# Hybrid encoder trunk: heavy and light experts strictly in turn, two more weight places, tables in small parts

## The chip, the cores and the metric

The kernel runs on one core of one Trainium2 chip. The metric is the time of one execution in device microseconds, lower is better. Times of a stage are counted from the first instruction of the profiled execution.

## What is computed

Two residual layers over 1024 tokens of width 1024. Each has a token mixer (layer 0: differential and latent attention side by side; layer 1: neighbourhood attention) and a mixture of 32 gated experts, and after both a layer norm. The change touches the mixture alone:

```python
grp = argmax(softmax(xt @ w_rg + b_rg))                     # 4 groups of 8 experts
top_v, top_i = top_k(e_logits of that group, 2)             # two experts per token
gate = softmax(top_v) * g_w
def block(tids, e, w):                                      # up to 128 tokens of one expert
    xb = x_pad[tids]
    hdn = silu(xb @ w1[e]) * (xb @ w3[e])                   # 1024 -> 512, twice
    return (hdn @ w2[e]) * w                                # 512 -> 1024
out = segment_sum(y, slot_tok)
```

All arrays are float32. An expert has 6 MB of weights (w1, w3, w2), a layer 192 MB, read once per execution.

## The kernel before

A layer first does its attention and output projection (`out_project`), on whose last rows the router works. Then `moe` walks through the 32 experts, one step `s` per expert. Experts are ranked by their number of tokens; a rank has a fixed room of slots (`ROOM`, 176 down to 24). Ranks 0 to 13, and rank 31, are heavy: 128 slots at a time, as three products of a split operand (each float32 operand as a rounded part `hi` and a rest `lo`, lines 164 to 169). Ranks 14 to 29, and 30, are light: 64 or 32 slots, plain float32 products straight from the loaded weights (`pair`, line 1165), two or four of them side by side on the array. The four largest ranks have an extra light block for what is over 128. Ranks 30 and 31 stand for the fixed experts 0 and 1; their weights can be loaded before the ranking is known.

A step has rounds `i` = 0 to 7 for gate and up of expert `s`, then 8 to 11 for the down product of expert `s - 1`. In between, at fixed rounds, stand the transposes of the next expert's tokens (`turn`, tiles `xs` or `xh`, `xl`), of the hidden row (`turn_hidden`, tiles `hs` or `hh`, `hl`), the gathers of tokens and the scatters of results. Instructions of TensorE, VectorE, ScalarE and GpSimd run in the order in which the code emits them; SyncE's queue is ordered by a scheduler, and works in that order.

For a heavy expert each 1 MB load is split into `hi` (ScalarE, line 2082) and `lo` (VectorE, line 2083) in two halves, called pieces; there are five places for pieces and the code splits three ahead (`fill`). A heavy expert's load place is free when its second piece is split, a light one's when TensorE has read it.

`Experts` sets the order of the experts (`order`: two fixed, `LEAD` light ones, then heavy ones with light ones spread between, `TRAIL` light ones last) and the list of 192 loads (`flow`). Loads go to SyncE's queue in that order (`load`, line 2103), each waiting for its place: nine common places (`raw`), shared with the output projection, and two more (`mw2`). The last 14 loads use the nine alone. The loads of expert numbers that only the ranking knows need a register, read by SyncE (line 2100).

`overflow_tables` (line 1337 on) computes tables for tokens beyond the room of their expert, all on VectorE; it is a generator, and `moe` calls `next(over)` in each round from step 8 on until it ends. It gives way three times.

Of the kernel before, what the change touches and what calls it, by code (L numbers as in the profile page):

```python
# [18 lines left out]
P = 128  # L19
# [20 lines left out]

FIRST_MORE = 6
LEAD, TRAIL, TURN = 1, 2, 6
# [92 lines left out]
class Kernel:  # L135
# [960 lines left out]
    def moe(self, layer, ahead):  # L1096
# [3 lines left out]
        with ExitStack() as st:  # L1100
# [33 lines left out]
            def turn(p):  # L1134
                for b, n, at in self.blocks(order[p]):
                    if n < P:
                        pt = flat(psT.tile([P, 4, P], F32, name="tp", tag="tp")).rearrange("p (c s) -> p c s", c=NC)
                        for c in range(NC):
                            nc.tensor.transpose(pt[:, c, 0:n], gx[b][at:at + n, c::NC], self.ident[at:at + n, at:at + n])  # L1139
                        xts[b] = pr.tile([P, NC, 64], F32, name="xs", bufs=3)[:, :, 0:n]  # L1140
                        nc.scalar.activation(xts[b], pt[:, :, 0:n], AF.Copy)  # L1141
                        continue
                    hi, lo = xts[b] = pr.tile([P, NC, P], F32R, name="xh"), pr.tile([P, NC, P], F32R, name="xl")
                    for g in range(2):
                        pt = psT.tile([P, 4, P], F32, name="tp", tag="tp")
                        for j in range(4):
                            c = 4 * g + j
                            nc.tensor.transpose(pt[:, j, 0:n], gx[b][0:n, c::NC], self.ident[0:n, 0:n])
                        self.split(hi[:, 4 * g:4 * g + 4], lo[:, 4 * g:4 * g + 4], pt[:, :, 0:n])

# [39 lines left out]
            def turn_hidden(p):  # L1190
                for b, n, _ in self.blocks(order[p]):
                    pt = psT.tile([P, 4, P], F32, name="tp", tag="tp")
                    for j in range(4):
                        nc.tensor.transpose(pt[:, j], hs[b][:, j::4], self.ident)  # L1194
                    if n == P:
                        hts[b] = [pr.tile([P, 4, P], F32R, name="hh"), pr.tile([P, 4, P], F32R, name="hl")]
                        self.split(hts[b][0], hts[b][1], pt)
                    else:

                        h = pr.tile([P, 4, 64], F32, name="hs", bufs=3)  # L1200
# [45 lines left out]
            turn(0)  # L1246
            for s in range(NE + 1):
                if s < NE:
# [5 lines left out]
                    for i in range(8):  # L1254
# [82 lines left out]
    def overflow_tables(self, keep, pr):  # L1337
# [8 lines left out]
        V.tensor_tensor(m, over[:, :, None].to_broadcast([P, NE, NT]), t[:, None, 0:NT].to_broadcast([P, NE, NT]), op=OP.is_gt)  # L1346
        blocks = kk([NE], "oblk")
        V.tensor_reduce(blocks, m, axis=AX.X, op=OP.add)
        end = blocks
        for d in (1, 2, 4, 8, 16):  # L1350
# [3 lines left out]
            end = e  # L1354
        begin = kk([NE], "obegin")
# [5 lines left out]
        for i in range(2):  # L1361
            m = pr.tile([P, NT, NE], F32, name="rt", tag="gs", bufs=1)
            at, st = kk([NT], "oat%d" % i), kk([NT], "ost%d" % i)
            V.tensor_tensor(m, self.ch[i], cap[:, None].to_broadcast([P, NT, NE]), op=OP.mult)
            V.tensor_reduce(at, m, axis=AX.X, op=OP.add)
            V.tensor_tensor(at, self.po[i], at, op=OP.subtract)
            V.tensor_tensor(m, self.ch[i], begin[:, None].to_broadcast([P, NT, NE]), op=OP.mult)
            V.tensor_reduce(st, m, axis=AX.X, op=OP.add)
            V.scalar_tensor_tensor(st, st, float(P), at, op0=OP.mult, op1=OP.add)
# [597 lines left out]
class Experts:  # L1967
# [3 lines left out]
    def __init__(self, k, layer, side):  # L1971
# [4 lines left out]
        self.more, self.first_more = None, FIRST_MORE  # L1976
# [58 lines left out]
    def tile(self, shape, name="raw"):  # L2035

        more = self.of_more()
        self.count += 1
        if more:
            return self.more.tile(shape, F32, name=name, tag="raw", bufs=RAWS2)  # L2040
        return self.raw(shape, name)

    def of_more(self):
        i = self.count - self.first_more
        return i >= 0 and i % (RAWS + RAWS2) < RAWS2 and self.count + 1 < len(self.flow) - TAIL

    def follow(self):

        while self.done < len(self.flow):
            held = self.held.get(self.of_more(), [])  # L2050
            n = RAWS2 if self.of_more() else RAWS
# [36 lines left out]
    def load(self, upto, mark=None):  # L2088
        k, nc = self.k, self.k.nc
        while self.done < min(upto, len(self.flow)):  # L2090
            p, j = self.flow[self.done]
            r = self.order[p]
            more = self.of_more()
# [54 lines left out]
```

## Time and profile before

| | |
|---|---|
| median of 3 runs | 2553.79 us (2548.26 to 2555.2) |
| profiled execution | 2551.09 us, of it span 2549.3 us |
| TensorE / VectorE / ScalarE busy | 2352.0 / 1601.5 / 1209.1 us |
| experts of layer 0: first and last product | 776.26, 1339.29 us |
| experts of layer 1: first and last product | 1941.47, 2496.17 us |

A share of busy time is an average over stages with different limits; the two expert stages are read on their own below. The granted clock is given as a share of full speed: 1.00 is 2.4 GHz, 0.50 is 1.2 GHz. The DMA share is the mean busy share of the core's 16 DMA engines, and can come out a little over 1.

### The profile page before, as it was taken

Reading aid. Unit: us, or ns where it says so; the run is one execution under the profiler, and the core shown is the slowest. Engines: PE = TensorE matmul, PEld = TensorE weight load, DVE = VectorE, ACT = ScalarE, POOL = GpSimd, SP = SyncE. Lnnn points to the kernel's source line nnn. Section 1 sums busy time; section 2 is a strip of 40 time slices with the busy share of each in tenths; the row PEclk is TensorE's granted clock in tenths of the full one; section 3 lists DMA queues with packets and bytes.
Section 4 is the critical chain, followed back from the end, with each engine's and each line's share of the span. In section 5 each row is a group of like instructions: output and inputs, shape, how many; then the busy total and the mean of one; then the engine's idle time right before and its main releaser. Section 6 shows DMA issues by size and latency. Waiting matters only on the chain. (4 is left out here: it accounts for less than half of the span.)

```text
span 2549.3 us, 34566 instructions
## 1 busy us (share of the span) xinstructions
PE 2352.0 (92%) x11972; PEld 1691.2 (66%) x11972; DVE 1601.5 (63%) x2923; ACT 1209.1 (47%) x2093; POOL 484.6 (19%) x513
## 2 busy tenths in 40 slices
PE   8998999999988999999986999999897999999991
PEld 8786777887774655656535878888784665666640
DVE  4328878888575665656645346676676565656656
ACT  3217866777213534444424346666413443444433
POOL 0006752332001111111111012222001111111112
PEclk9999999999998989999997999999998999999995
DMA  4105412000626898999996564545735898999996
GB/s 147 40 17 100 87 39 75 1 1 25 241 101 229 336 391 336 395 406 409 391 402 234 163 147 126 127 127 157 250 115 181 306 392 358 404 402 416 402 414 245
DMA packets 179754, 582.12 MB, mean 228 GB/s; under 512 B 32728, under 2 KB 91112, under 8 KB 128632
## 3 DMA queue, kind: packets, MB, share of 16 engines
q1 hardware_dynamic: 165880, 546.29, 59.1%
q0 software_dynamic: 13696, 33.58, 3.7%
q8 instruction: 97, 1.59, 0.2%
q14 instruction: 81, 0.66, 0.1%
HBM read 518.61 MB, written 56.05 MB: 225 GB/s over the span
## 5 line engine op out<-in xcount | busy, mean ns | idle before, releaser
L2083 DVE TENSOR_TENSOR lo<-raw,hi 128x1024 fp32r<-128x1024 f32 x360 | 423.9, 1222 | 84.3 <-ACT hi L2082 79.2
L2082 ACT ACTIVATE hi<-raw 128x1024 fp32r<-128x1024 f32 x360 | 363.7, 1057 | 43.2 <-PE hy L169 34.1
L1165 PE MATMUL hy<-raw,xs 128*64 128x512 f32 (+1 forms) x1408 | 302.3, 615 | 7.0 <-DMA raw<-in_w_up_dram 3.1
L1232 POOL DMA_INDIRECT y_scratch<-xg,msi x72 | 71.8, 997 | 895.2 <-DVE xg L1226 767.8
L1226 DVE SCALAR_TENSOR_TENSOR xg<-hy,mgate,xg 128x512 f32<-128x512 f32 (+2 forms) x172 | 125.3, 745 | 129.0 <-PE hy L1165 115.8
L168 PE MATMUL hy<-lo,xh 128*128 128x512 f32 x480 | 190.0, 396 | 8.2 <-DVE lo L2083 8.2
L167 PE MATMUL hy<-hi,xh 128*128 128x512 f32 x480 | 197.1, 411 | 0.0
L169 PE MATMUL hy<-hi,xl 128*128 128x512 f32 x480 | 189.6, 395 | 0.0
L1165 PEld LDWEIGHTS hy<-raw,xs 128*64 128x64 f32 (+1 forms) x1408 | 80.4, 132 | 159.4 <-issue 137.0
L1165 PE MATMUL hy<-raw,hs 128*64 128x512 f32 (+1 forms) x704 | 144.8, 608 | 11.7 <-DMA raw<-in_w_down_dram 10.2
L161 DVE TENSOR_TENSOR pl<-tp,ph 128x512 fp32r<-128x512 f32 x192 | 129.9, 680 | 23.9 <-ACT ph L160 23.8
L160 ACT ACTIVATE ph<-tp 128x512 fp32r<-128x512 f32 x192 | 112.3, 595 | 40.6 <-PE tp L664 23.4
L167 PE MATMUL o<-whi,xh 128*128 128x512 f32 (+1 forms) x320 | 126.5, 395 | 2.6 <-ACT whi L160 2.5
L168 PE MATMUL o<-wlo,xh 128*128 128x512 f32 (+1 forms) x320 | 125.6, 392 | 1.6 <-DVE wlo L161 1.6
L169 PE MATMUL o<-whi,xl 128*128 128x512 f32 (+1 forms) x320 | 124.7, 390 | 2.2 <-DVE xl L152 2.2
L167 PEld LDWEIGHTS hy<-hi,xh 128*128 128x128 f32 x480 | 91.4, 190 | 33.5 <-issue 10.0
L1764 POOL TENSOR_SCALAR e<-e,sm 128x288 f32<-128x288 f32 (+1 forms) x128 | 68.7, 549 | 218.5 <-DVE sm L1763 202.0
L161 DVE TENSOR_TENSOR pt<-tp,pt 96x384 fp32r<-96x384 f32 (+1 forms) x128 | 65.2, 549 | 70.9 <-ACT pt L160 69.5
L168 PEld LDWEIGHTS hy<-lo,xh 128*128 128x128 f32 x480 | 91.2, 190 | 27.6 <-DVE lo L2083 11.3
L151 ACT ACTIVATE hh<-tp 128x512 fp32r<-128x512 f32 x30 | 17.9, 597 | 185.5 <-PE tp L1194 185.5
L657 POOL TENSOR_SCALAR e<-e,sm 128x1024 f32<-128x1024 f32 x64 | 72.1, 1126 | 177.5 <-DVE sm L656 111.9
L1141 ACT ACTIVATE xs<-tp 128x512 f32<-128x512 f32 (+1 forms) x44 | 23.4, 537 | 173.0 <-PE tp L1139 173.0
(429 smaller groups left out, 5578.3 us busy)
## 6 DMA issues: line engine op xcount, KB each, us to landing
raw<-in_w_gate_dram SPq DMA_DIRECT2D x128, 1024.0 KB, 14.9
raw<-in_w_up_dram SPq DMA_DIRECT2D x128, 1024.0 KB, 13.3
raw<-in_w_down_dram SPq DMA_DIRECT2D x128, 1024.0 KB, 14.6
y<-y_scratch SPq DMA_DIRECT2D x14, 1024.0 KB, 13.1
v_scratch<-vst SPq DMA_DIRECT2D x32, 256.0 KB, 3.4
raw<-in_odd_w_qkv_dram SPq DMA_DIRECT2D x16, 512.0 KB, 5.4
vw<-v_scratch SPq DMA_DIRECT2D x16, 512.0 KB, 4.9
x_scratch<-z SPq DMA_DIRECT2D x14, 512.0 KB, 2.8
```

Source lines behind the costliest of these rows:

```text
L160: nc.scalar.activation(hi, src, AF.Copy)
L161: return lambda: nc.vector.tensor_tensor(lo, src, as32(hi), op=OP.subtract)
L167: mm(out, l[0], r[0], start=start, stop=False)
L168: mm(out, l[0], r[1], start=False, stop=False)
L169: mm(out, l[1], r[0], start=False, stop=stop)
L657: nc.gpsimd.tensor_scalar(e, e, sm[:, 3:4], 1.0, op0=OP.mult, op1=OP.mult)
L1165: mm(out[at:at + n], x[:, k], ws(k)[i], start=k == z, stop=k == nk - q + z, tile_position=(0, at))
L1226: nc.vector.scalar_tensor_tensor(x, y, gate, x, op0=OP.mult, op1=OP.add))
L1232: nc.gpsimd.indirect_dma_start(out=self.y_dram, out_offset=bass.IndirectOffsetOnAxis(ap=slot(b, n)[1], axis=0), in_=yo[0:n], in_offset=Non ...
L1764: nc.gpsimd.tensor_scalar(e, e, sm[:, 2:3], 1.0, op0=OP.mult, op1=OP.mult)
L2082: nc.scalar.activation(hi, src, AF.Copy)
L2083: nc.vector.tensor_tensor(lo, src, as32(hi), op=OP.subtract)
```

## The change

The order of the experts becomes (H heavy, L light; B one of the four largest, with an extra block):

```
before  L H L B H L H L H L B L H L H L H L B L H L H L B L H L H L L L
after   L H L B L H L H L H L B L H L H L H L B L H L H L B L H L H L L
```

`TRAIL` goes from 2 to 1. The places `xh`, `xl`, `hh` and `hl` go from two to one each, `xs` and `hs` from three to two. A third pool `mw3` of two 1 MB places opens in the same room of memory; of 13 loads 9 go to the common places, 2 to `mw2`, 2 to `mw3`. The twelve static loads no longer wait for the ranking; the first load by number waits for the last activation of `turn(0)`. `overflow_tables` gives way fourteen times, and is called in every second round from step 4 on.

```diff
-LEAD, TRAIL, TURN = 1, 2, 6
+RAWS3, THIRD = 2, 5
+LEAD, TRAIL, TURN = 1, 1, 6
...
-            ex.load(ex.static - 2)
-            ex.load(ex.static, self.ranked)
             pr = self.pool("mr", bufs=2, ctx=mr, side="right")
+            ex.third = self.pool("mw3", bufs=RAWS3, ctx=mr, side="right")
+            ex.load(ex.static)
...
-                    hi, lo = xts[b] = pr.tile([P, NC, P], F32R, name="xh"), pr.tile([P, NC, P], F32R, name="xl")
+                    hi, lo = xts[b] = [pr.tile([P, NC, P], F32R, name=x, bufs=1) for x in ("xh", "xl")]
...
-                        hts[b] = [pr.tile([P, 4, P], F32R, name="hh"), pr.tile([P, 4, P], F32R, name="hl")]
+                        hts[b] = [pr.tile([P, 4, P], F32R, name=x, bufs=1) for x in ("hh", "hl")]
...
-            turn(0)
+            ex.load(ex.static + 1, turn(0))
...
-                        elif s >= 8:
+                        elif s >= 4 and i % 2:
                             next(over, None)
...
+    def which(self):
+        i = self.count - self.first_more
+        if i < 0 or self.count + 1 >= len(self.flow) - TAIL:
+            return 0
+        i %= RAWS + RAWS2 + RAWS3
+        return 1 if i < RAWS2 else 2 if THIRD <= i < THIRD + RAWS3 else 0
```

Three places show how instructions move. The first is SyncE's queue at the start of the experts of layer 0 (`x_scratch<-z` writes the last token rows that the first gathers read; `idsi` holds the ranked expert numbers). Before:

```order
L2103 DMA raw<-in_w_down_dram 128x2048 [waits PE_49]
L2103 DMA raw<-in_w_down_dram 128x2048 [waits DMAHW2_49,PE_49]
L849 DMA x_scratch<-z 128x512 [waits DVE_49,Pool_49]
L849 DMA x_scratch<-z 128x512 [waits DMAHW4_49,Pool_49]
L2103 DMA raw<-in_w_down_dram 128x2048 [waits DVE_49,PE_49]
L2100 TENSOR_LOAD idsi [waits DVE_49]
```

After:

```order
L2119 DMA raw<-in_w_down_dram 128x2048 [waits PE_49]
L2119 DMA raw<-in_w_down_dram 128x2048 [waits DMAHW2_49,PE_49]
L2119 DMA raw<-in_w_down_dram 128x2048 [waits PE_49]
L851 DMA x_scratch<-z 128x512 [waits DMAHW4_49,DVE_49,Pool_49]
L851 DMA x_scratch<-z 128x512 [waits Pool_49]
L2119 DMA raw<-in_w_down_dram 128x2048 [waits DMAHW6_49,Activation_49]
L2116 TENSOR_LOAD idsi [waits DVE_49]
```

The third load moves ahead of the writes of z, and the fourth from behind 15 reads of numbers to ahead of all of them; the first load by number, which stood behind 15 reads, stands behind 23.

The second is VectorE where the tables begin (`lo` is a piece's rest, `xg` the sum of a result, `hl` and `xl` the rests of a heavy expert's operands). Before, in step 8:

```order
L2083 TENSOR_TENSOR lo<-raw,hi 128x1024 x5
L1343 TENSOR_TENSOR over<-total,cap 128x32
L1345 TENSOR_SCALAR capt<-iota 128x8
L1346 TENSOR_TENSOR rt<-over,capt 128x256
L1348 TENSOR_REDUCE oblk<-rt 128x32
L1352 COPY oend_8681<-oblk 128x1
L1353 TENSOR_TENSOR oend_8681<-oblk 128x31
```

After, in step 4:

```order
L1186 TENSOR_TENSOR hg<-hg,hy 128x512
L1347 TENSOR_TENSOR over<-total,cap 128x32
L1349 TENSOR_SCALAR capt<-iota 128x8
L1350 TENSOR_TENSOR rt<-over,capt 128x256
L1229 SCALAR_TENSOR_TENSOR xg_7394<-hy,mgate,xg_7394 64x512 x2
L154 TENSOR_TENSOR hl<-tp,hh 128x512
L1214 TENSOR_TENSOR hs<-hs,tp 128x256
L1353 TENSOR_REDUCE oblk<-rt 128x32
L1357 COPY oend_8117<-oblk 128x1
L1358 TENSOR_TENSOR oend_8117<-oblk 128x31
```

Sixteen instructions stood in one block; now three stand alone, and other work of the step comes before the next part.

The third is TensorE at the end of the experts of layer 0 (`xs` and `hs` are the light operands, `hg` a hidden row, `xg` a token row). Before:

```order
L1165 MATMUL hy<-raw,xs 32x512 x4
L1194 MATMUL tp<-ident,hg 128x128 x4
L1165 MATMUL hy<-raw,xs 32x512 x8
L1139 MATMUL tp<-ident,xg_7394 128x32 x8
L1165 MATMUL hy<-raw,xs 32x512 x4
L1165 MATMUL hy<-raw,hs 32x512 x8
L1165 MATMUL hy<-raw,xs 32x512 x4
L1194 MATMUL tp<-ident,hg 128x128 x4
L1165 MATMUL hy<-raw,xs 32x512 x12
L1165 MATMUL hy<-raw,hs 32x512 x4
L1194 MATMUL tp<-ident,hg 128x128 x4
L1165 MATMUL hy<-raw,hs 32x512 x12
```

After:

```order
L169 MATMUL hy<-hi,hh 128x512
L170 MATMUL hy<-lo,hh 128x512
L171 MATMUL hy<-hi,hl 128x512
L1168 MATMUL hy<-raw,xs 32x512 x4
L1197 MATMUL tp<-ident,hg 128x128 x4
L1168 MATMUL hy<-raw,xs 32x512 x12
L1168 MATMUL hy<-raw,hs 32x512 x4
L1197 MATMUL tp<-ident,hg 128x128 x4
L1168 MATMUL hy<-raw,hs 32x512 x12
```

The down products of the last heavy expert now end one light expert later in the list, so two light experts' products follow its gate and up instead of three.

## Rows read from the trace of the kernel before

**Rows 1.** Busy time by stretches, layer 0; the first line names the columns

```profile
core 0: us, PE busy (x) PEld busy (x) DVE busy (x) ACT busy (x) POOL busy (x), PEclk, DMA share, GB/s
796.00:816.00 20.00, 20.00 (x100) 13.53 (x100) 8.12 (x19) 6.98 (x10) 2.89 (x3) 1.00 0.74 258
...
840.00:860.00 20.00, 20.00 (x93) 10.64 (x92) 11.65 (x13) 9.74 (x12) 2.40 (x2) 1.00 0.61 219
...
942.00:948.00 6.00, 6.00 (x19) 4.23 (x19) 1.04 (x1) 1.08 (x2) 0.00 (x0) 0.50 1.01 418
948.00:954.00 6.00, 6.00 (x23) 1.86 (x24) 1.44 (x2) 0.00 (x0) 0.00 (x0) 0.76 0.74 267
...
980.00:1000.00 20.00, 20.00 (x98) 10.08 (x96) 3.97 (x6) 4.31 (x7) 1.95 (x2) 1.00 0.68 259
1020.00:1260.00 240.00, 238.05 (x1153) 145.49 (x1151) 149.24 (x162) 111.59 (x142) 37.02 (x32) 0.99 1.01 401
1284.00:1340.00 56.00, 43.88 (x244) 17.41 (x242) 22.37 (x30) 11.29 (x20) 6.05 (x6) 0.91 1.00 401
```

**Rows 2.** ScalarE in order of time: start, duration, instruction, idle before

```profile
1025.88 0.59 ACT L1182 ACTIVATE hg<-hy 128x512 f32<-128x512 f32 x1
...
1038.04 1.08 ACT L151 ACTIVATE xh<-tp 128x512 fp32r<-128x512 f32 x2 [1.65 <-PE tp L1148]
...
1056.70 0.59 ACT L1182 ACTIVATE hg<-hy 128x512 f32<-128x512 f32 x1
```

**Rows 3.** Weight loads issued from 1020 to 1260 us, by line

```profile
L2103 SPq DMA_DIRECT2D raw<-in_w_up_dram x29: 332/333/333, 1020.1 to 1256.6; - x29
...
L2103 SPq DMA_DIRECT2D raw<-in_w_gate_dram x29: 332/333/1117, 1022.4 to 1258.9; - x29
...
L2103 SPq DMA_DIRECT2D raw<-in_w_down_dram x28: 332/333/336, 1030.6 to 1249.4; - x28
```

**Rows 4.** Busy time by stretches, layer 1

```profile
1976.00:2040.00 64.00, 63.02 (x301) 38.63 (x300) 38.41 (x41) 30.65 (x39) 6.39 (x6) 1.00 0.82 307
...
2104.00:2108.00 4.00, 2.84 (x6) 1.74 (x6) 3.76 (x11) 0.00 (x0) 3.26 (x3) 0.57 1.01 428
...
2440.00:2497.00 57.00, 46.68 (x259) 21.45 (x257) 24.87 (x35) 13.18 (x23) 7.58 (x7) 0.91 0.93 385
```

**Rows 5.** VectorE in order of time, first and last of 34 table instructions

```profile
928.66 0.18 DVE L1343 TENSOR_TENSOR over<-total,cap 128x32 f32<-128x32 f32 x1
...
940.55 0.17 DVE L1372 TENSOR_SCALAR oat<-oat 128x8 f32<-128x8 f32 x1
```

**Rows 6.** TensorE in order of time, waits for pieces in both layers

```profile
938.16 0.80 PE L168 MATMUL hy<-lo,xh 128*128 128x512 f32 x1 [2.95 <-DVE lo L2083]
...
941.96 0.79 PE L168 MATMUL hy<-lo,xh 128*128 128x512 f32 x1 [0.87 <-DVE lo L2083]
...
2104.40 0.71 PE L168 MATMUL hy<-lo,xh 128*128 128x512 f32 x1 [2.93 <-DVE lo L2083]
...
2108.20 0.50 PE L168 MATMUL hy<-lo,xh 128*128 128x512 f32 x1 [0.96 <-DVE lo L2083]
```

**Rows 7.** SyncE's queue in order of time, start of layer 0's experts

```profile
768.37 10.78 SPq L2103 DMA_DIRECT2D raw<-in_w_down_dram  x2
```

**Rows 8.** SyncE's reads of expert numbers, both layers: ns min/median/max

```profile
L2100 SPq TENSOR_LOAD <-idsi x60: 260/266/477, 770.0 to 1954.8; - x60
L2100 SPq FUSED_REGOPS  x60: 147/147/192, 770.5 to 1955.2; - x60
```

**Rows 9.** TensorE's last four waits in each layer, first and last

```profile
1329.92 1.07 PE L1165 MATMUL hy<-raw,hs 128*32 128x512 f32 x8 [0.68 <-DMA raw<-in_w_down_dram]
...
1337.35 1.94 PE L1165 MATMUL hy<-raw,hs 128*32 128x512 f32 x8 [1.37 <-DMA raw<-in_w_down_dram]
...
2487.80 1.06 PE L1165 MATMUL hy<-raw,hs 128*32 128x512 f32 x8 [0.62 <-DMA raw<-in_w_down_dram]
...
2495.11 1.06 PE L1165 MATMUL hy<-raw,hs 128*32 128x512 f32 x8 [1.32 <-DMA raw<-in_w_down_dram]
```

More of the change, by code (lines that the diff above doesn't have):

```diff
@@ L1134, in turn @@
             def turn(p):
+                mark = None
                 for b, n, at in self.blocks(order[p]):
@@ L1139, in turn @@
                             nc.tensor.transpose(pt[:, c, 0:n], gx[b][at:at + n, c::NC], self.ident[at:at + n, at:at + n])
[L1140 to L1141 removed]
+                        xts[b] = pr.tile([P, NC, 64], F32, name="xs", bufs=2)[:, :, 0:n]
+                        mark = nc.scalar.activation(xts[b], pt[:, :, 0:n], AF.Copy)
                         continue
[L1143 removed]
+                    hi, lo = xts[b] = [pr.tile([P, NC, P], F32R, name=x, bufs=1) for x in ("xh", "xl")]
                     for g in range(2):
@@ L1149, in turn @@
                         self.split(hi[:, 4 * g:4 * g + 4], lo[:, 4 * g:4 * g + 4], pt[:, :, 0:n])
+                return mark
             def product(out, x, c, w, start, stop):
@@ L1346, in overflow_tables @@
         V.tensor_tensor(m, over[:, :, None].to_broadcast([P, NE, NT]), t[:, None, 0:NT].to_broadcast([P, NE, NT]), op=OP.is_gt)
+        yield
         blocks = kk([NE], "oblk")
@@ L1354, in overflow_tables @@
             end = e
+            if d in (2, 8):
+                yield
         begin = kk([NE], "obegin")
@@ L1364, in overflow_tables @@
             V.tensor_tensor(m, self.ch[i], cap[:, None].to_broadcast([P, NT, NE]), op=OP.mult)
+            yield
             V.tensor_reduce(at, m, axis=AX.X, op=OP.add)
             V.tensor_tensor(at, self.po[i], at, op=OP.subtract)
+            yield
             V.tensor_tensor(m, self.ch[i], begin[:, None].to_broadcast([P, NT, NE]), op=OP.mult)
+            yield
             V.tensor_reduce(st, m, axis=AX.X, op=OP.add)
+            yield
             V.scalar_tensor_tensor(st, st, float(P), at, op0=OP.mult, op1=OP.add)
@@ L1975, in __init__ @@
         self.pool = k.pool("mw", bufs=RAWS, ctx=self.ctx, side=side)
-        self.more, self.first_more = None, FIRST_MORE
+        self.more, self.first_more, self.third = None, FIRST_MORE, None
         self.pieces, self.filled, self.halves = {}, 0, {}
@@ L2035, in tile @@
     def tile(self, shape, name="raw"):
-        more = self.of_more()
+        which = self.which()
         self.count += 1
-        if more:
-            return self.more.tile(shape, F32, name=name, tag="raw", bufs=RAWS2)
+        if which:
+            pool, n = ((self.more, RAWS2), (self.third, RAWS3))[which - 1]
+            return pool.tile(shape, F32, name=name, tag="raw", bufs=n)
         return self.raw(shape, name)
-    def of_more(self):
+    def which(self):
         i = self.count - self.first_more
-        return i >= 0 and i % (RAWS + RAWS2) < RAWS2 and self.count + 1 < len(self.flow) - TAIL
+        if i < 0 or self.count + 1 >= len(self.flow) - TAIL:
+            return 0
+        i %= RAWS + RAWS2 + RAWS3
+        return 1 if i < RAWS2 else 2 if THIRD <= i < THIRD + RAWS3 else 0
     def follow(self):
         while self.done < len(self.flow):
-            held = self.held.get(self.of_more(), [])
-            n = RAWS2 if self.of_more() else RAWS
+            held = self.held.get(self.which(), [])
+            n = (RAWS, RAWS2, RAWS3)[self.which()]
             if len(held) >= n and held[-n] not in self.used:
@@ L2092, in load @@
             r = self.order[p]
-            more = self.of_more()
+            more = self.which()
             t = self.tile([P, 4, 512] if j < 4 else [P, 2, D])
```

2 lines of the change are left out of this document (1 added, 1 removed).

## Prediction

> **What bounds the kernel now.** I read the page's first two parts, then the busy time by stretches, then who waits in the stretches where TensorE is not busy, then the weight loads' own issues. Nearly all of the change lies in the two expert stages (layer 0: 776 to 1339 us, layer 1: 1941 to 2496 us), so only they are priced.
>
> Inside a stage two engines are almost equally loaded. TensorE is busy in 238.05 of the 240 us from 1020 to 1260 while the DMA share is 1.01 [rows 1]. One heavy and one light expert take TensorE 30.8 us there, by the silu of two heavy experts that follow each other [rows 2]; they need twelve 1 MB loads. In the same 240 us 29 + 29 + 28 = 86 loads are issued [rows 3], one per 2.79 us, so twelve take 33.5 us. The stream of weights is therefore the slower of the two by 2.7 us a pair, and lives on the lead it had before 1020. When that is gone TensorE waits: from 1284 to 1340 it is busy 43.88 of 56 us [rows 1], in layer 1 46.68 of 57 us [rows 4]. The lead could have been larger: the DMA share is 0.74, 0.61 and 0.68 in 796-816, 840-860 and 980-1000 [rows 1], 5.2 + 7.8 + 6.4 = 19.4 us idle with work to do; layer 1 idles 0.18 x 64 = 11.5 us in 1976-2040 alone [rows 4]. In these stretches the loads wait for places, that is for TensorE. A lead gained early is spent late, microsecond for microsecond, until TensorE itself has no waits left.
>
> **The change part by part.**
>
> *Tables in fifteen parts.* Before, all of it stands in the first three rounds of step 8, a heavy expert: between 928.66 and 940.72 us VectorE works off 34 small instructions [rows 5], in three blocks, and the subtractions that TensorE needs stand behind them. TensorE waits 2.95 + 0.87 us in layer 0 and 2.93 + 0.96 us in layer 1 [rows 6]. Its clock then falls: granted 0.50 in 942-948 and 0.76 in 948-954, TensorE busy throughout [rows 1], 3.0 + 1.4 = 4.4 us of work lost; in layer 1 0.57 in 2104-2108 with 2.84 us busy [rows 4], 1.2 us. After, the parts hang on every second round of steps 4 to 7, at most about 1 us each. VectorE's cover: it is busy 149.24 of 240 us [rows 1], so four steps of some 15.4 us leave 23 us free for the table work, some 8 us (the 12.06 us less what else VectorE does in them). Steps 5 and 7 are heavy and carry some 1.9 and 1.1 us of it; splitting runs three pieces ahead, so I take nothing for the cost. Bounds: nothing to those 8 us per layer, were all of it exposed again. Gain of the part: 3.8 + 4.4 = 8.2 us in layer 0, 3.9 + 1.2 = 5.1 us in layer 1.
>
> *Two more places.* From the start of the stage each place that comes free is filled by a load two further on in the list. While the loads wait for places this is a lead of two loads, 2 x 2.79 = 5.6 us per layer. Bounds: nothing, if TensorE alone set the end; no more than 5.6.
>
> *Strict turns.* Behind the third expert, each (heavy, light) pair becomes (light, heavy), the one touching pair of heavy experts goes, and two trailing light experts are left in place of three. TensorE's sum is the same. The light expert, quicker on TensorE, gives its places back first, up to six loads earlier for part of a pair; the gain in lead lies between 0 and two loads (5.6 us). I take 3 us, the middle: the shares of 0.61 to 0.74 and the 1.01 [rows 1] are one extreme each.
>
> *Start of the stage.* The third w_down load goes ahead of the two writes of z on SP's queue, the fourth directly behind them. The third needs only a place from the output projection's last products; the pair in the row at 768.37 was held to that time and, with the row's 10.78 us, to 779 us [rows 7]. The first gathers then have the queues to themselves. What could be lost: 23 instead of 15 reads of expert numbers stand ahead of the first numbered load, 8 more at 0.27 + 0.15 us and what lies between [rows 8], some 4 us. That load serves the third expert, which TensorE reaches after two whole ones, and the places for the loads behind it come free only when TensorE has used them. Net between -2 and +4 us per layer; I take 0.
>
> *Single places.* The split input of a heavy expert is written at 1038.04 us; the products that last read the place ended at 1025.88 us, when the silu of the heavy expert before begins [rows 2]: 12 us of slack, a light expert's share. With a light expert between any two heavy ones, no write meets a reader; xs and hs with two places in place of three are reused at the earliest a whole step after their last reader, the extra blocks of the four largest experts counted. Cost: nothing if so, bounds under the slower rival.
>
> *The sum.* Seen from the stream, layer 0 ends 8.2 + 5.6 + 3 = 16.8 us sooner, and 19.4 us of idle DMA stand against that, so it has the room; layer 1 5.1 + 5.6 + 3 = 13.7 us. Seen from TensorE, what can go is the waits and the low clock. Late in layer 0: 56 - 43.88 - 0.7 (after the end) = 11.4 us of waits, of which the last four, for the last experts' own w_down (4.2 us, first and last in [rows 9]), stay, so 7.2; with 8.2 and some 2 of the 4 us lost by the clock of 0.91 over 43.88 us, 17.4 us. Layer 1: 57 - 46.68 - 0.8 = 9.5, less the last four (4.1 us, [rows 9]) 5.4, with 5.1 and 2: 12.5 us. The smaller of each pair counts: 16.8 + 12.5 = 29.3 us. From the profiled execution's 2551.09 us (span 2549.3 and 1.8 around it) that gives 2521.8 us. The runs' median, 2553.79, is 2.7 us above that execution, so the forecast is 2524 us.
>
> A rule speaks against it. The rows show 401 GB/s over 240 us, with a full DMA share [rows 1]. The Trainium skill (DMA: Bandwidth & Descriptors, "Specifications" and "Where 436 GB/s comes from") puts what one core gets from HBM at about 358 GB/s. As an estimate from that page, 201 MB of weights per layer would take 562 us, the whole stage, and no order or place could gain anything; the trace disagrees, 401 being above the page's bound.
>
> **The rivals.**
>
> *The stream keeps the end, and only its head start counts.* If the stream is saturated right behind the start, TensorE's earlier progress at 940 finds no idle DMA to use, and the layer gains the two places alone: 2 x 5.6 = 11.2 us, 2553.8 - 11 = 2543 us. For it: shares of 1.01 over 240 us. Against it: 0.68 in 980-1000, after the stall [rows 1]. Chance 0.13.
>
> *Nothing moves.* The lead is lost again, because the last 14 loads use the nine common places only, as before: the stream then idles late for places, and what is won at the start is given back. From 1284 to 1340 the share is still 1.00 [rows 1], which is against it as long as TensorE waits for loads. Time: 2553, gains of a few us inside the spread. Chance 0.06. The rule on HBM of the Trainium skill, weighed above, would end here too; of the chance it has 0.01.
>
> *Slower: single places are too few.* If the write of xh or hh has to wait until the reader's whole step is through, each heavy expert shows its two copies (1.08 us in the row, [rows 2]) and about as long for the subtractions behind them, some 2 us, before its first product: 14 experts x 2 layers x 2 = 56 us against 29 gained, 2580 us. It decides from the point where the write comes less than those 2 us before the first product. For it: only one place. Against it: the 12 us of slack above. The Trainium skill (Trainium Kernel Development and Optimization, "Best Practices") advises double buffering; by that rule this would be the outcome, and the order of the experts is why I don't follow it. With a fresh VectorE wait in the heavy steps 5 and 7 as the milder form: chance 0.06.
>
> **How the numbers follow.** The forecast's own chance is 0.75, with 2511 (every wait and low clock of both layers gone) to 2539 (half the sum) as its own range. A measurement of this kernel can tell 0.3%, 7.7 us, from no change, that is below 2546. The forecast and most of the first rival lie below: faster 0.84. Same 0.10: a weak first rival and the second. Slower 0.06. The range for eight in ten is 2509 to 2547: below by the forecast's own end and a little for the start of the stage, above to the far side of the first rival, with about 0.12 left above.
>
> **What would show each step.** Right: no TensorE wait for "lo" of over 1 us near step 8 and no granted clock of 0.5 there; the DMA share in 796-1020 and its twin in layer 1 nearer to 1; TensorE's waits for "raw" in the last 55 us of each stage at about 4 us; each stage 12 to 18 us shorter; all else unchanged. Wrong: those late waits as long as before (the first rival), DMA shares below 0.95 in the last 100 us (the second), or waits for xh, xl, hh or hl that come back with every heavy expert (the third).

## The result, and the profile after

The changed kernel takes 2524.15 us in the median (2523.08 to 2526.13, 4 runs) beside 2551.03 us for the kernel before on the same chip (2544.44 to 2555.2, 4 runs), a ratio of 0.990 [0.989, 0.992]. The profiled execution took 2523.08 us, with a span of 2521.3 us. The forecast was 2524 us.

First each expert stage as a whole, from its first to its last product. The columns are the stretch, its length, busy time of TensorE, its weight loads, VectorE, ScalarE and GpSimd with their instructions, the granted clock, the DMA share and GB/s. Layer 0 and layer 1 of the kernel before:

```profile
776.26:1339.29 563.03, 543.90 (x2596) 318.55 (x2596) 336.08 (x435) 237.94 (x308) 77.34 (x69) 0.97 0.95 370
1941.47:2496.18 554.71, 537.41 (x2596) 316.47 (x2596) 335.52 (x435) 237.44 (x308) 76.69 (x69) 0.98 0.94 374
```

The same of the kernel after:

```profile
777.69:1323.22 545.53, 534.65 (x2596) 315.82 (x2596) 334.54 (x435) 237.67 (x308) 78.10 (x69) 0.98 0.97 380
1925.26:2468.46 543.20, 532.31 (x2596) 315.83 (x2596) 334.51 (x435) 237.37 (x308) 79.40 (x69) 0.99 0.96 380
```

Length less busy time is what TensorE waits: 19.1 us before and 10.9 after in layer 0, 17.3 and 10.9 in layer 1. The 2596 products are the same. That their busy time falls, by 9.3 and 5.1 us, goes with the granted clock, which rises from 0.97 to 0.98 and from 0.98 to 0.99; two digits can't tell whether the clock is all of it. Together the stages lose 17.5 and 11.5 us. In layer 0 the stage begins later, though: from the start of ScalarE's last work on `z` to the first product it is 23.6 us in place of 21.8. That leaves 27.2 us, and the profiled executions differ by 28.0.

Now the stretches that answer to [rows 1] and [rows 4], in the same columns: the places of the idle DMA in layer 0, the low clock behind step 8, the long middle, the last 56 us of layer 0, and the last 57 us of layer 1.

```profile
796.00:816.00 20.00, 20.00 (x97) 13.11 (x97) 9.46 (x22) 8.61 (x12) 2.89 (x3) 1.00 0.77 269
840.00:860.00 20.00, 20.00 (x95) 11.51 (x95) 7.20 (x11) 4.91 (x7) 2.47 (x2) 1.00 0.72 273
942.00:948.00 6.00, 6.00 (x30) 5.04 (x29) 5.39 (x7) 3.58 (x5) 0.94 (x1) 1.00 1.02 427
980.00:1000.00 20.00, 20.00 (x94) 10.17 (x94) 4.93 (x6) 3.86 (x6) 2.15 (x2) 1.00 0.93 376
1020.00:1260.00 240.00, 237.37 (x1156) 146.15 (x1154) 149.04 (x164) 112.03 (x145) 39.28 (x34) 0.99 1.01 399
1268.00:1324.00 56.00, 49.74 (x292) 27.09 (x284) 35.97 (x44) 22.50 (x32) 7.83 (x7) 0.95 1.00 401
2412.00:2469.00 57.00, 50.98 (x310) 28.92 (x309) 36.41 (x45) 23.23 (x34) 8.72 (x8) 1.00 0.95 387
```

The clock in 942 to 948 is 1.00 in place of 0.50, the share in 980 to 1000 is 0.93 in place of 0.68, in 840 to 860 only 0.72 in place of 0.61. The middle is as full as before. In the last stretch of layer 0 TensorE is busy 49.7 us in place of 43.9, in layer 1 51.0 in place of 46.7. What waits are left there is seen in TensorE in order of time, which answers to [rows 9]; of the last four waits of each layer the first and the last stand here, and of those before them the two longest in layer 0:

```profile
1260.07 0.50 PE L169 MATMUL hy<-hi,xh 128*128 128x512 f32 x1 [0.74 <-ACT hi L2098]
1261.33 0.50 PE L170 MATMUL hy<-lo,xh 128*128 128x512 f32 x1 [0.76 <-DVE lo L2099]
...
1313.39 1.06 PE L1168 MATMUL hy<-raw,hs 128*32 128x512 f32 x8 [1.14 <-DMA raw<-in_w_down_dram]
...
1321.28 1.94 PE L1168 MATMUL hy<-raw,hs 128*32 128x512 f32 x8 [0.69 <-DMA raw<-in_w_down_dram]
...
2459.51 1.07 PE L1168 MATMUL hy<-raw,hs 128*32 128x512 f32 x8 [0.78 <-DMA raw<-in_w_down_dram]
...
2467.39 1.07 PE L1168 MATMUL hy<-raw,hs 128*32 128x512 f32 x8 [1.29 <-DMA raw<-in_w_down_dram]
```

The last four sum to 4.3 and 4.8 us, as before (4.2 and 4.1). Before them, in the last 70 us of the stage, the waits are 2.7 us in layer 0 and 2.2 in layer 1, where there were 7.2 and 5.4. All waits of these 70 us are called the late waits below: 11.4 and 9.5 us before, 7.0 and 7.0 after. The lead of the weight stream lasts nearly to the end.

One thing was not foreseen, at the start of layer 0. TensorE in order of time in the kernel before:

```profile
774.41 1.65 PE L1139 MATMUL tp<-ident,xg 64*128 64x64 f32 x16 [3.26 <-DMA xg<-x_scratch,fgi]
```

and ScalarE there:

```profile
755.86 1.98 ACT L1113 ACTIVATE xg<-ones 128x1024 f32<-128x1024 f32 x2
766.29 3.89 ACT L1113 ACTIVATE xg<-ones 128x1024 f32<-128x1024 f32 x4 [8.44 <-PE lg L974]
...
775.63 1.06 ACT L1141 ACTIVATE xs<-tp 128x512 f32<-128x512 f32 x2
```

TensorE of the kernel after:

```profile
771.82 1.66 PE L1141 MATMUL tp<-ident,xg 64*128 64x64 f32 x16 [1.28 <-DMA xg<-x_scratch,fgi]
777.69 1.98 PE L1168 MATMUL hy<-raw,xs 128*64 128x512 f32 x4 [4.21 <-ACT xs L1143]
```

and its ScalarE:

```profile
765.94 5.78 ACT L1114 ACTIVATE xg<-ones 128x1024 f32<-128x1024 f32 x6 [10.32 <-PE lg L976]
...
773.27 3.88 ACT L2098 ACTIVATE hi<-raw 128x1024 fp32r<-128x1024 f32 x4
777.06 1.06 ACT L1143 ACTIVATE xs<-tp 128x512 f32<-128x512 f32 x2
```

The tokens arrive 2.6 us sooner. But two of the six zero fills of `xg` have moved from 755.86 to 765.94, behind a routing product. An experiment below shows that the smaller pools do that; that these tiles then lie elsewhere in memory, and wait there for an earlier user of the room, is an inference. Four splits of pieces stand between the fills and the copy `xs` that the first product needs, and TensorE waits 4.2 us (3.2 us in layer 1).

### The profile page after: what moved, and what is told of

It reads as the page before. It is cut to its first block, busy times and chain, and to the rows that moved or that the text cites. A ratio compares the mean times of both kernels' runs of the same rounds, so it can differ in the third digit from the quotient of the medians.

```text
span 2521.3 us, 34562 instructions
## 1 busy us (share of the span) xinstructions
PE 2335.7 (93%) x11972; PEld 1686.9 (67%) x11972; DVE 1599.7 (63%) x2923; ACT 1209.2 (48%) x2093; POOL 486.9 (19%) x513
## 5 line engine op out<-in xcount | busy, mean ns | idle before, releaser
L1168 PE MATMUL hy<-raw,xs 128*64 128x512 f32 (+1 forms) x1408 | 293.1, 608 | 7.9 <-ACT xs L1143 7.4
L1229 DVE SCALAR_TENSOR_TENSOR xg<-hy,mgate,xg 64x512 f32<-64x512 f32 (+2 forms) x172 | 125.0, 745 | 116.0 <-PE hy L1168 110.5
L163 DVE TENSOR_TENSOR pl<-tp,ph 128x512 fp32r<-128x512 f32 x192 | 129.9, 680 | 23.7 <-ACT ph L162 23.6
L1186 DVE TENSOR_TENSOR hg<-hg,hy 128x512 f32<-128x512 f32 x30 | 20.7, 689 | 147.8 <-PE hy L171 147.8
L1126 POOL DMA_INDIRECT xg<-x_scratch,mgi x68 | 88.8, 1306 | 89.9 <-DVE mgate L1078 34.8
## 6 DMA issues: line engine op xcount, KB each, us to landing
y<-y_scratch SPq DMA_DIRECT2D x14, 1024.0 KB, 13.3
```

The source lines that it names most:

```text
L163: return lambda: nc.vector.tensor_tensor(lo, src, as32(hi), op=OP.subtract)
L1126: nc.gpsimd.indirect_dma_start(out=x[0:n], out_offset=None, in_=self.x1_dram, in_offset=bass.IndirectOffsetOnAxis(ap=self.first[:, p:p + 1 ...
L1168: mm(out[at:at + n], x[:, k], ws(k)[i], start=k == z, stop=k == nk - q + z, tile_position=(0, at))
L1229: nc.vector.scalar_tensor_tensor(x, y, gate, x, op0=OP.mult, op1=OP.add))
```

## The experiments

Each kernel is the one before or the one after with one or more parts changed. The stages are the lengths of the profiled execution, the start is the time from the start of ScalarE's last work on `z` to the first product of layer 0 and of layer 1. The kernel before had medians of 2550.1 to 2551.8 us beside them.

| kernel | median us | ratio to before | stages us | start us |
|---|---|---|---|---|
| before | 2551.0 | 1 | 563.0, 554.7 | 21.8, 21.6 |
| tables in parts alone | 2537.4 | 0.994 [0.991, 0.996] | 553.7, 553.1 | 22.2, 21.6 |
| strict turns alone | 2528.1 | 0.990 [0.987, 0.993] | 551.1, 545.3 | 22.1, 21.6 |
| places alone | 2539.8 | 0.995 [0.993, 0.997] | 554.7, 548.6 | 23.6, 21.6 |
| tables and turns | 2528.55 | 0.991 [0.988, 0.994] | 550.1, 547.0 | 22.1, 21.6 |
| the same, single operand places | 2534.4 | 0.994 [0.993, 0.996] | 551.1, 547.6 | 23.6, 21.6 |
| after | 2524.15 | 0.990 [0.989, 0.992] | 545.5, 543.2 | 23.6, 21.6 |
| after, old tables | 2523.9 | 0.989 [0.986, 0.993] | 546.1, 543.9 | 23.6, 21.6 |
| after, old turns | 2529.8 | 0.992 [0.989, 0.994] | 548.5, 546.0 | 23.6, 21.6 |
| after, earlier start | 2523.25 | 0.989 [0.986, 0.993] | 552.6, 542.9 | 19.6, 18.8 |
| and later splits | 2515.8 | 0.986 [0.984, 0.989] | 545.6, 544.1 | 19.6, 18.8 |
| after again, beside it | 2522.6 | 0.989 [0.987, 0.991] | 544.6, 540.3 | 23.6, 21.6 |
| splits a round sooner | 2516.5 | 0.987 [0.985, 0.989] | 545.7, 540.4 | 19.6, 18.7 |
| later splits again, beside it | 2520.7 | 0.988 [0.987, 0.990] | 546.2, 542.4 | 19.4, 18.6 |

What lies between the two stages varied between 599 and 606 us among kernels that don't differ there, so the stages leave out a part of the noise. But each is of a single execution, and the two executions of the changed kernel differ by 0.9 us in layer 0 and 2.9 in layer 1: a difference of that size between two rows shows nothing.

**Tables in parts alone.**

```diff
-                        elif s >= 8:
+                        elif s >= 4 and i % 2:
```

with the eleven further `yield`s that the change puts into the tables.

> The kernel before with the tables in fifteen parts, and nothing else of the change. Theory (TensorE's waits at step 8 and the low clock behind them make places come free late, and there is idle DMA behind them, so the whole delay reaches the end): 13 us faster, 8 in layer 0 and 5 in layer 1; no wait for lo of over 1 us near step 8. Rival (the stream of weights is saturated and keeps the end, only its head start counts): within 3 us of the kernel before, the time gained at step 8 coming back as longer waits for raw in the last 55 us of each stage.

Measured: 14 us less. No wait for `lo` is left near step 8. The late waits are 9.3 and 11.8 us. By the medians the term of 13.3 us holds for this part alone. By the stages of the profiled execution, the slowest of its six, it is 9.4 us in layer 0 and only 1.6 in layer 1, where 8.2 and 5.1 were predicted. In layer 1 the 3.9 us of waits at step 8 are gone, but the late waits are 2.3 us longer than before: in this execution the rival's mechanism is at work there, beside the theory's. The stages in the columns of above:

```profile
775.40:1329.07 553.67, 540.44 (x2596) 318.81 (x2596) 334.86 (x434) 238.28 (x308) 77.12 (x69) 0.98 0.96 376
1933.82:2486.90 553.08, 537.41 (x2596) 316.19 (x2596) 335.22 (x435) 237.94 (x308) 77.31 (x69) 0.98 0.95 376
```

**Strict turns alone.**

```diff
-LEAD, TRAIL, TURN = 1, 2, 6
+LEAD, TRAIL, TURN = 1, 1, 6
```

> The kernel before with one trailing light expert less (strict turns), and nothing else. Step 8 is a light expert now, so the old tables in one go stand in a light step. Theory: the turns alone 3 us per layer, and if the block of tables in a light step no longer delays pieces also the 13 us of the tables, together 19 us faster; if it still does, 6 us faster. Rival (stream keeps the end): within 3 us of the kernel before.

Measured: 23.7 us less, nearly all that the whole change gives. The prediction's 6 us are refuted as the worth of this part alone; the other value that was expected, 19 us with the stall gone, was nearer. The reason stands in the order of the experts: with `TRAIL` at 1 the list from the fifth expert on moves by one place, and the ninth expert, step 8, is a light one. The table block is where it was, but it stands beside a light expert's work; TensorE shows no wait for `lo` near it. How much of the 23.7 us is the stall is told by the experiments below.

**Places alone.** The third pool, the single places and the loads at the start, with the old order and the old tables:

```diff
+RAWS3, THIRD = 2, 5
...
+            ex.third = self.pool("mw3", bufs=RAWS3, ctx=mr, side="right")
...
+                    hi, lo = xts[b] = [pr.tile([P, NC, P], F32R, name=x, bufs=1) for x in ("xh", "xl")]
```

> The change without the new order and without the parts of the tables: two more places, single places for heavy operands, the loads of the start as in the change. Two heavy experts are neighbours once per layer (steps 3 and 4), where a single place makes the second wait for the first. Theory: the lead of two loads, 11 us faster, less up to 2 us per layer at the neighbours; the waits for lo at step 8 of 3.8 us stay. Rival (stream keeps the end, only the head start counts): 11 us faster as well. Rival (single places are too few): slower than the kernel before, with waits for xh or hh at many heavy experts.

Measured: 12 us less, as expected, though the stall at step 8 is still there. The rival of the stream had 11 us for this kernel too, so this run does not tell the two apart. TensorE in order of time:

```profile
942.49 0.50 PE L170 MATMUL hy<-lo,xh 128*128 128x512 f32 x1 [2.94 <-DVE lo L2092]
946.29 0.50 PE L170 MATMUL hy<-lo,xh 128*128 128x512 f32 x1 [2.14 <-DVE lo L2092]
```

So the gain doesn't come from there; the late waits fall to 7.7 and 6.3 us.

**Tables and turns, without the places.**

> Tables in parts and strict turns, with the eleven places and the double operand places of before. Theory: 13 + 6 = 19 us faster; what it lacks to the change's 27 us is the price of the two places. Rival (only the head start of the stream counts): within 3 us of the kernel before.

Measured: 2528.55 us, where turns alone gave 2528.1. The tables add nothing to the turns. The stages:

```profile
775.74:1325.87 550.13, 533.02 (x2596) 314.55 (x2596) 334.74 (x434) 238.14 (x308) 76.36 (x69) 0.99 0.96 379
1924.89:2471.91 547.02, 532.97 (x2596) 314.65 (x2596) 334.54 (x435) 237.52 (x308) 76.62 (x69) 0.99 0.96 380
```

Beside the tables alone, TensorE's busy time is 7.4 and 4.4 us less; its waits are 3.9 us more in layer 0 and 1.6 less in layer 1. So what the order adds here shows as busy time, with a higher clock, more than as shorter waits. The late waits are 13.2 and 9.4 us here and 7.0 and 7.0 with the whole change: this is what the two more places take away.

**Single operand places.** The kernel before this one, with

```diff
-                    hi, lo = xts[b] = pr.tile([P, NC, P], F32R, name="xh"), pr.tile([P, NC, P], F32R, name="xl")
+                    hi, lo = xts[b] = [pr.tile([P, NC, P], F32R, name=x, bufs=1) for x in ("xh", "xl")]
```

and the same for `hh` and `hl`; `xs` and `hs` with two places.

> The kernel with the tables in parts and the strict turns on eleven places (2528.55 us), with single places for the heavy operands (xh, xl, hh, hl) and two for xs and hs, but without the two more weight places. My theory: with a light expert between any two heavy ones no write meets its reader, so nothing is lost: 2526 to 2531 us, stages within 1 us of 550.1 and 547.0. Rival (single places are too few): some 2 us for each of 28 heavy experts, up to 2580 us, with waits for xh or hh that come back with every heavy expert. A milder rival: the places cost 2 to 6 us, which the two more weight places then hide in the whole change.

Measured: 2534.4 us, 5.9 more by the medians, which were measured on two chips and whose intervals (as ratios to the kernel before) overlap. Inside the stages 1.0 and 0.6 us are lost, no more than two executions of one kernel differ, and 1.5 us at the start of layer 0, where the zero fills move as in the whole change: the narrower pools do that, not the third one. The rest, some 1 to 3 us (the profiled executions differ by 4.3 us), lies outside the stages and is not settled. None of it is a wait for a reader. ScalarE's group that writes `xh` (instructions, busy time, mean ns, idle before and what ended it), in this kernel:

```profile
L151 ACT ACTIVATE xh<-tp 128x512 fp32r<-128x512 f32 x30 | 16.2, 593 | 33.6 <-PE tp L1148 33.6
```

All of its waits end with `tp`, the transposed tokens that it copies. The milder rival's 2 to 6 us can't be excluded by the medians, but no wait for a reader is there to cause them. With the third pool and the loads of the start on top (this kernel against the changed one) the stages are 5.6 and 4.4 us shorter, 10 us as against 11.2 predicted for the two more places.

**After, with the old tables.**

```diff
-                        elif s >= 4 and i % 2:
+                        elif s >= 8:
```

with three breaks in place of fourteen.

> The whole change, but with the tables as before, in three blocks from step 8. My theory now: with strict turns step 8 is a light step, whose work needs no split pieces, so the block hides behind it: 2523 to 2528 us, no wait for lo of over 1 us near step 8. By the prediction's own terms (8.2 + 5.1 us for the tables) it would be 2535 to 2538 us, with waits for lo of some 3 us in step 8 or in the heavy step behind it.

Measured: 2523.9 us, equal to the whole change. VectorE works off the first and the last instruction of the block here:

```profile
926.89 0.19 DVE L1347 TENSOR_TENSOR over<-total,cap 128x32 f32<-128x32 f32 x1
...
937.01 0.17 DVE L1376 TENSOR_SCALAR oat<-oat 128x8 f32<-128x8 f32 x1
```

10.3 us, somewhat less than the 12.1 of before [rows 5], and TensorE meanwhile (stretches as above):

```profile
925.00:935.00 10.00, 10.00 (x48) 3.86 (x48) 8.12 (x31) 3.52 (x6) 0.85 (x1) 1.00 1.02 376
935.00:940.00 5.00, 5.00 (x26) 2.60 (x23) 4.79 (x11) 3.35 (x6) 1.07 (x2) 1.00 1.00 418
```

It is busy in every microsecond, at full clock, until 938.6 us with a light expert's products and transposes. With strict turns, the parts of the tables are worth nothing that these runs can show.

**After, with the old turns** (`TRAIL` 2).

> The whole change, but with the pairs (heavy, light) and three trailing light experts of before; the tables stand in parts, so the stall at step 8 is gone either way. My theory (lead that is worth only what TensorE still waits): order adds 4 to 8 us over tables and places, so 2528 to 2533 us. By the prediction's own term of 3 us a layer it is 2530 us; if terms were independent and the order worth the 23.7 us that it gave alone, 2548 us. Heavy operands with single places meet here once, where two heavy experts touch: there a wait of up to 2 us may show.

Measured: 2529.8 us, as expected: over tables and places the order is worth 5.7 us. It also shows what a single place does when two heavy experts touch. ScalarE's group of `xh`, first as a group:

```profile
L153 ACT ACTIVATE xh<-tp 128x512 fp32r<-128x512 f32 x30 | 16.3, 593 | 39.9 <-PE tp L1150 36.2 <-PE hy L170 3.7
```

and the one row behind its last figure, in order of time:

```profile
853.61 1.08 ACT L153 ACTIVATE xh<-tp 128x512 fp32r<-128x512 f32 x2 [3.72 <-PE hy L170]
```

There the copy waits 3.7 us for the product that reads the place (and 3.7 us in layer 1). TensorE shows no wait for `xh` behind it, so even this single meeting was covered.

**After, with an earlier start.** Zero fills of the first two token places first, the first expert's transposes and copy ahead of the first pieces' splits:

```diff
-            ex.fill(AHEAD)
             ex.load(ex.static + 1, turn(0))
+            for x in xgs[4:]:
+                zero(x)
+            ex.fill(AHEAD)
+            for x in xgs[2:4]:
+                zero(x)
```

> The whole change, with the start of the stage put in another order: the zero fills of the first two token places first, those of the last two behind the first expert's tokens, those of the third and fourth behind the first pieces; the first expert's transposes and their copy ahead of the first pieces' splits. My theory: the first expert's copy xs then follows its tokens directly, at about 773 to 774 us instead of 777.1, so the first product comes some 3 us earlier in each layer and the stage ends as much earlier: 2517 to 2521 us. Rival: the stream of weights sets the end and the loads behind the start come no sooner, so the 3 us come back as late waits: 2523 to 2525 us. A second rival: the splits come later instead and the heavy third expert waits for them, 2525 to 2530 us.

Measured: 2523.25 us, nothing gained, though the start is 4.0 and 2.8 us shorter. The time is the first rival's, but none of the expectations had the reason. TensorE in order of time:

```profile
789.32 0.23 PE L1053 MATMUL hy<-rhs,xg 128*128 128x160 bf16 x1 [1.96 <-DVE xg L1047]
```

a stretch behind it, in the columns of the stretches above:

```profile
790.00:798.00 8.00, 8.00 (x27) 3.25 (x28) 5.30 (x21) 0.00 (x0) 0.00 (x0) 0.57 0.62 258
```

and VectorE, which it waited for:

```profile
779.94 4.63 DVE L2104 TENSOR_TENSOR lo<-raw,hi 128x1024 fp32r<-128x1024 f32 x4 [6.04 <-ACT hi L2103]
...
788.91 1.52 DVE L1047 TENSOR_SCALAR xg<-iotab,po 128x192 bf16<-128x192 bf16 x8
```

The four subtractions now stand ahead of the tables of the first expert, VectorE is idle 6 us before them, and the tables come late. TensorE waits 2.0 us, and its clock is 0.57 for 8 us in which it is busy throughout, 3.4 us of work lost. Together that is more than the start had won in layer 0. In layer 1 the same wait is 1.6 us, and the stage is no longer than with the change (542.9 and 543.2 us).

**Earlier start and later splits.** The call of `fill` before the loop is left out, and within it

```diff
-                        ex.fill((s, i), AHEAD)
+                        if s or i == 7:
+                            ex.fill((s, i), AHEAD)
```

> The kernel with the earlier start of the stage, and besides the first pieces' splits go behind the routing tables' work of the first expert (issued in its last round). My theory: in the earlier start the four subtractions (4.63 us on VectorE) stood ahead of the tables that TensorE reads at 787 us, so it waited 1.96 us there, its clock fell to 0.50 until 797, and the 3.5 to 4 us of the start were given back. With the splits behind, that wait is gone, the granted clock stays at 1.00 from 790 to 798, and the pieces are still ready before the heavy second expert begins at about 800. So the first product at 774 to 775 us is kept to the end of the stage: 3 us per layer less than the changed kernel, 2517 to 2520 us. Rival: the stream of weights keeps the end, the 3 us come back as late waits: 2523 to 2525 us. A second rival: the two weight places that the first pieces hold come free some 4 us later and loads start late, which costs 1 to 5 us: 2524 to 2528 us.

Measured: 2515.8 us (2514.4 to 2520.2), beside

> The whole change once more, beside the kernel with the earlier start on the same chip, so that the two can be compared directly: 2522 to 2526 us.

which gave 2522.6 us (2519.5 to 2525.1). The same products:

```profile
785.42 0.24 PE L1053 MATMUL hy<-rhs,xg 128*128 128x160 bf16 x1
```

and the same stretch:

```profile
790.00:798.00 8.00, 7.30 (x37) 3.42 (x33) 4.67 (x5) 5.36 (x7) 0.00 (x0) 1.00 0.33 97
```

The wait is gone and the clock is 1.00, as the theory said; the start's gain is kept, with 545.6 and 544.1 us for the stages beside the change's 545.5 and 543.2. What is new in the row is a DMA share of 0.33: the splits came only at 793.5 us, and two weight places were held until then.

**The splits a round sooner** (`i >= 6` in place of `i == 7`), the last kernel beside it.

> The earlier start with the first pieces' splits one round sooner, ahead of the second expert's tokens. In the run before, the splits came at 793.5 us, behind the copy xh; the two weight places that they hold were kept to 799, no load was issued from 784.8 to 794.8 and the DMA share was 0.33 in 790 to 798. My theory: the splits now stand at about 779 to 788, the loads behind them are issued by 790, the share there rises to over 0.9, the wait of 0.70 us for lo goes. Of the lead won (up to 0.67 x 8 = 5.4 us of the stream) only the late waits can be given back, 7.1 and 5.0 us, of which some 4 are the last experts' own w_down and stay: 1 to 4 us over both layers less than the run before, 2511 to 2515 us. Rival: the stream idles a little later instead (places come back with TensorE's pace), 2515 to 2517 us. A second rival: TensorE waits at 797 for the second table, which now stands behind the subtractions on VectorE: 2517 to 2520 us.

> The earlier start with the splits in the first expert's last round once more, beside the one with the splits a round sooner: 2514 to 2518 us.

Measured: 2516.5 us (2514.7 to 2521.2) and 2520.7 us (2514.6 to 2523.8). The stretch became what was expected,

```profile
790.00:798.00 8.00, 8.00 (x41) 3.77 (x37) 1.32 (x3) 1.68 (x3) 0.00 (x0) 1.00 0.96 383
```

but the time did not follow: 2516.5 us is outside the 2511 to 2515 that were expected, and in the first rival's range. Whether the earlier splits gain anything can't be told, as the two ranges overlap and the second kernel, which missed its 2514 to 2518 here, had 2515.8 us on the other chip. Nine runs of it have a median of 2516.9 us, ten of the changed kernel 2523.25. Both early kernels are some 6 us below the change, by medians over all runs; the intervals of their ratios to the kernel before overlap in part with the change's.

## Why the prediction was right, and where its steps were not

*The sum seen from TensorE* was 17.4 and 12.5 us of waits and low clock that can go; 17.5 and 11.5 went. For layer 0 the forecast took the stream's 16.8, which is 0.6 less. So the size of what TensorE can lose was right, and it rests on a few rows: how long TensorE is not busy, and where its clock is low. Its parts were not right. Of waits 11.0 and 9.3 us were to go (7.2 + 3.8 and 5.4 + 3.9), and 8.2 and 6.4 went, as the late waits fell by 4.4 and 2.5 only. Of low clock 6.4 and 3.2 us were to come back, and busy time fell by 9.3 and 5.1. The two errors are of one size and opposite, so that the sums agree within 1 us is in part luck; a second profiled execution of the changed kernel has stages that are 0.9 and 2.9 us shorter still. That the time itself came out within 0.2 us is luck too: 29.3 us were forecast and 26.9 measured, and the forecast set out from 2553.79 us, a median of three runs, where the four runs beside the changed kernel have 2551.03.

*Tables in parts:* 13.3 us predicted, 14 measured alone by the medians (11 by the stages, with 1.6 of 5.1 in layer 1), but 0 in the change as made. The step that failed is that the stall was put down to the tables' block alone. It needs a heavy expert beside the block, and the order of the experts, which the prediction read for touching pairs only, puts a light one there. Two of the change's parts remove the same stall, each when alone, and the prediction counted it once, under the one that adds nothing where the other stands.

*Strict turns:* 6 us predicted for the lead, 23.7 measured alone, which by subtraction is the stall's 14 us and 9 more. Where the stall is gone anyway, they are worth 8.9 us without the places (2537.4 less 2528.55, measured side by side) and 5.7 with them. So the size of 6 us was near. With the places the reason, a longer lead, shows too: the late waits are 11.8 and 8.0 us with the old turns and 7.0 and 7.0 with strict ones. Without the places it does not: there the late waits go from 9.3 and 11.8 to 13.2 and 9.4 us, and it is TensorE's busy time that falls. Why it does stays open; a part may be chance, as the clock behind short waits differs between executions (last section).

*Two more places:* 11.2 us predicted, 12 measured with the single places and the loads at the start, 10 by the stages of one execution each over single places alone, but 4.4 by the medians over tables and turns. The price of the narrow pools is in the last figure.

*In order:* tables, then turns, then places give 14.4, 8.9 and 4.4 us, 27.7 together, where the terms said 13.3, 6 and 11.2. Each alone gives 14, 24 and 12, a sum of 50. That the tables and the turns share the stall is shown. That the places, which give 12 us alone and 4.4 last, share something with the other two is seen in these times only; what it is, beside the price of the narrow pools, is not shown.

*Start of the stage:* 0 predicted, between -2 and +4. It lost 1.8 us in layer 0, by a way not thought of (the zero fills). The last kernels show that 4.0 and 2.8 us were to be had in the same place.

*Single places:* no wait for a reader, as predicted; the move of the zero fills is theirs. The Trainium skill (Trainium Kernel Development and Optimization, "Best Practices") advises to double-buffer so that DMA overlaps with compute. These places are written by ScalarE and VectorE, not by DMA, so that the advice asks for two of them was the prediction's reading and not the page's word. The trace has no such wait with strict turns, and one of 3.7 us per layer without them. The slower rival's price was mis-sized a little: the order has 15 heavy experts per layer, not 14, so its 56 us would be 60.

*The rivals.* That the stream keeps the end, with 2543 us, is refuted for the change by its 2524 us and by the effects of the tables and the order, which are no head start; in layer 1 of the tables alone, though, more than half of the waits saved at step 8 came back as late waits. That nothing moves is refuted by the late waits of 7.0 us in place of 11.4 and 9.5. The Trainium skill (DMA: Bandwidth & Descriptors, "Specifications") gives a limit of about 358 GB/s for one core's share of the HBM, a stack's 716 GB/s divided by two cores. Taken as a bound for this kernel, which runs on one core, it would have allowed no gain; the stretch from 1020 to 1260 shows 399 GB/s after, and the measurement decides.

*What was to be seen.* No wait for `lo` and no clock of 0.5 near step 8: seen. Waits for `raw` of about 4 us in the last 55 us: 4.8 and 4.8. Stages 12 to 18 us shorter: 17.5 and 11.5. A DMA share nearer to 1 early: in part. In layer 0 it rose from 0.88 to 0.93 over 796 to 1000, most of it behind step 8; in layer 1 the twin of [rows 4] hardly moved. Layer 0 before, then layer 0 and layer 1 after:

```profile
796.00:1000.00 204.00, 198.23 (x902) 120.75 (x902) 119.87 (x165) 88.14 (x112) 27.33 (x25) 0.96 0.88 335
...
796.00:1000.00 204.00, 202.04 (x951) 120.79 (x951) 119.39 (x168) 88.64 (x113) 28.18 (x25) 1.00 0.93 361
...
1960.00:2024.00 64.00, 63.02 (x300) 33.35 (x299) 36.04 (x53) 26.32 (x34) 6.35 (x6) 1.00 0.83 304
```

The prediction said that the loads wait for TensorE in the early stretches. In 796 to 816 of the kernel before that is only half of it. SyncE's waits there (in total, times, longest):

```profile
SPq L2103 <- PE hy L1165: 11.4, 2, 6.2
SPq L2103 <- DVE lo L2083: 11.3, 2, 9.6
```

As much is a wait for VectorE, whose split of a piece frees a heavy expert's place. After the change it is still 10.1 of 16.6 us, and the share of this stretch rose from 0.74 to 0.77 only.

What stays open is the 1 to 3 us of the narrow pools outside the stages, why strict turns without the places lower TensorE's busy time, and whether the splits a round sooner gain anything.

## What to carry to other kernels

Where several edits remove idle time of one engine, sum what that engine can still lose, by stretches, and take the edits' own terms only up to it. Check the waits and the clock in that sum one by one afterwards, since a right total can hide two errors. Before a stall is put down to a block of work, look at what stands beside it in the order, since a change of order may move the victim instead of the block. A gain at the start of a stage is real only when the next thing that the early engine will need has been brought forward too: look for who is idle before it.

## What the runs showed of the hardware that was not expected

A wait of 2.0 us of TensorE at 787 us was followed by a granted clock of 0.57 over 8 us of unbroken work, a mean: from 791 to 797 it was 0.50, the level of 1.2 GHz. In the next kernel, without the wait, the same stretch had 1.00. The clock cost more than the wait, 3.4 us against 2.0.

A shorter wait can go either way. In layer 1 of the changed kernel TensorE waits 0.98 us for `xl` at 2114 us, in both of its profiled executions. The stretch behind it, first in the one, then in the other:

```profile
2117.00:2122.00 5.00, 5.00 (x16) 3.87 (x15) 3.47 (x3) 3.48 (x5) 0.00 (x0) 0.66 1.01 374
...
2117.00:2122.00 5.00, 5.00 (x23) 4.13 (x22) 4.44 (x4) 4.66 (x6) 0.00 (x0) 1.00 1.03 378
```

The same kernel lost 1.7 us by the clock in one execution and nothing in the other. Such waits come back four times per layer, before and after the change, so single executions can differ by that much without any edit.

From 1020 to 1260 us DMA moved 399 to 401 GB/s in all fourteen traces of this case, before and after; what changed is when the stream of weights stands still, not its pace.
